# Loading scale, shift and the first product's weights interleaved by k-tile, with eight blocks of that product beside the load

## The chip, the cores and the metric

The kernel runs on one core of one Trainium2 chip. The metric is the device time of one execution in microseconds (us), the median of several runs. Differences of about 0.2% can be measured here.

## The reference

Two layers work on x (256 tokens, 2048 channels, float32), both conditioned on a vector c. From c come, for each layer, six vectors of 2048 (shift, scale and gate, twice):

```
mod = silu(c) @ w_ada[i] + b_ada[i]
sh1, sc1, gt1, sh2, sc2, gt2 = split(mod, 6)
h = rms_norm(x, pre_mix_g[i]) * (1.0 + sc1) + sh1
y = conformer_conv(h, ...)        # layer 0
...
x = x + gt1 * rms_norm(y, post_mix_g[i])
h = rms_norm(x, pre_ffn_g[i]) * (1.0 + sc2) + sh2
x = x + gt2 * rms_norm(swiglu_ffn(h, ...), post_ffn_g[i])
```

The convolution module of layer 0 is `u = h @ w_pw1 + b_pw1` (2048 to 4096), `a * sigmoid(g)` of its halves, a causal depthwise convolution with 31 taps over the tokens, layer norm, silu, and a second product `@ w_pw2`. Layer 1 has gated linear attention in its place. Both end in a SwiGLU network of width 5632.

## The kernel before, in words

**Layout.** Channels lie on the partitions, tokens along the free axis: x is 16 k-tiles of 128x256. Weights stream in tiles of 1 MB, each holding 16 blocks of 128x128 in the order in which they are multiplied (`ORDERS`). ScalarE rounds each half tile to `hi` (L282), and GpSimd or VectorE makes `lo = raw - hi` (L283; GpSimd for all of pw1, the first product). A block is multiplied as hi times the activation's high half, hi times its low half, and lo times the high half: L314, L315 and L320 for a block with a bank half of 256 columns. There are three buffers for `hi` and three for `lo` (half tiles), and six for `raw`.

**Modulation vectors.** For shift and scale of the first layer (`ada` tiles) VectorE multiplies a tile of w_ada by silu(c) and accumulates along its free axis (L261); one tile gives one column, 128 values of mod. A bias is added (L267), and for a scale `chunk_done` makes `(1 + scale) * gain` (L204). `modulate` then makes the k-tile of h: VectorE (L388, which reads the spread root of x from PSUM), ScalarE (L391, the high half), VectorE (L392, the low half). Three other vectors of layer 0 (`adap` tiles) are made on TensorE (L215).

**The order of the work.** `tile_order` writes out one list of all transfers, issued by SP in that order: the 16 scale tiles, with the parameters behind the second and x behind the third of them; then the 16 shift tiles, with the first four tiles of pw1 among them; then the other 28 tiles of pw1 with 26 `adap` tiles spread between them, 10 more `adap` tiles, and the rest. The bias of the scale and its product with the gain come once, over 16 columns, when all 16 scale tiles are there; the shift is finished column by column. Within an engine, instructions are ordered ahead of time by the compiler's own schedule.

**The first product.** `block_order` puts the first `PW1_GROUP` = 4 of the 32 output blocks together: for each k, all four, so that they advance as h becomes ready. The other 28 blocks follow one by one, each over all 16 k. Output blocks come as pairs, 0 and 16, 1 and 17 and so on (value and gate of one channel tile). Each block has its own bank of PSUM out of four (`mm`). `conv_done` reads a finished block on ScalarE (L549 for the value, L554 for the gate's sigmoid; two buffers each), multiplies them into `up` (L556; on VectorE for the first two channel tiles, else on GpSimd; four buffers), and VectorE runs the taps one after the other in PSUM (L597, two buffers; for the last two tiles L578 with part of the taps on TensorE, L565). Behind the last tile stand the layer norm's statistics, its root on GpSimd (L354), and the second product.

Of the kernel before, what the change touches and what calls it, by code (L numbers as in the profile page):

```python
# [14 lines left out]
P = 128  # L15
# [12 lines left out]
EPS = 1e-6  # L28
GROUP = 4
# [11 lines left out]
PW1_GROUP = 4  # L41
# [11 lines left out]
def ffn_in_obs(half):  # L53
# [4 lines left out]
    "pw1": block_order(PW1_OBS, KD, PW1_GROUP),  # L58
# [24 lines left out]
def tile_order():  # L83
# [11 lines left out]
    order = ada(0, SC1)  # L95
    order[2:2] = [("par", 0, 0)]
    order[4:4] = [("x", 0, 0)]
    shift = ada(0, SH1)
    order += shift[:4] + pw1[:1] + shift[4:7] + pw1[1:2] + shift[7:10] + pw1[2:3] + shift[10:13] + pw1[3:4] + shift[13:]
    order += spread(pw1[PW1_GROUP:], late[:26]) + late[26:36]  # L100
# [23 lines left out]
def trunk(ctx: ExitStack, tc: tile.TileContext, a: dict, out: bass.AP):  # L124
# [74 lines left out]
    def chunk_done(layer, chunk):  # L199
        m = modcol(layer, chunk * KD, KD)  # L200
        kinds = {SC1: (0, "pre_mix_g"), GT1: (1, "post_mix_g"), SC2: (2, "pre_ffn_g"), GT2: (3, "post_ffn_g")}
        if chunk in kinds:
            kind, g = kinds[chunk]
            nc.vector.scalar_tensor_tensor(  # L204
                out=der[:, layer * 4 + kind, :], in0=m, scalar=1.0 if kind in (0, 2) else 0.0,
                in1=cols(g, layer * KD, KD), op0=ALU.add, op1=ALU.mult,
            )
# [30 lines left out]
    def pump_one():  # L238
# [19 lines left out]
        if kind == "ada":  # L258
# [5 lines left out]
            if i % KD == KD - 1 or (name, i // KD) == (0, SH1):  # L264
                first = i if i // KD == SH1 and name == 0 else i - KD + 1
                m = modcol(name, first, i + 1 - first)
                nc.vector.tensor_tensor(  # L267
                    out=m, in0=m, in1=cols("b_ada", name * 6 * KD + first, i + 1 - first), op=ALU.add
                )
                if i % KD == KD - 1:  # L270
                    chunk_done(name, i // KD)
            if (name, i // KD) == (0, SH1):
                modulate(i % KD, rbx, 0, 0, SH1)
# [27 lines left out]
    def product(name, kts, act, on_done, step=None, narrow=(), join=True):  # L301
        live = {}
        for idx, (ob, k) in enumerate(ORDERS[name]):
            if idx % HALF == 0:
                w_hi, w_lo = next_half()
            if ob not in live:
                live[ob] = [ps.tile([P, 512], F32, tag="mm", name=f"{name}_{ob}"), 0]
            acc, n = live[ob]
            s = slice((idx % HALF) * P, (idx % HALF + 1) * P)
            pair = act(k)  # L310
            x_hi, x_lo = pair[:, 0, :], pair[:, 1, :]
# [12 lines left out]
            if end:  # L324
                live.pop(ob)
                on_done(ob, acc[:, :T] if ob in narrow else joined(ob, acc) if join else acc)
                if step is not None:
                    step()
# [600 lines left out]
```

## Time and profile before

| What | Value |
|---|---|
| Median of 3 runs | 2474.18 us (2470.78 to 2474.72) |
| Span of the profiled execution | 2464.2 us |
| Own time of the profiled execution | not given beside the span; the median is 9.98 us above the span |
| Mean granted TensorE clock | 0.983 |
| TensorE / VectorE / ScalarE / GpSimd busy | 95% / 75% / 45% / 11% of the span |
| DMA | 604.32 MB, mean 245 GB/s |

Times in the profile are microseconds from the span's start. "Busy" of TensorE counts matmuls that overlap, so one of 0.28 us may follow another after 0.12. A row of the timeline is: start, duration, engine, line, operation, what it writes and reads, how many are merged, and in brackets how long the engine had been idle and what released it. A row of a group is: count, then total busy time and mean nanoseconds of one, then idle time ahead of them and who ended it. A row of a stretch gives its bounds, its length, then busy time of TensorE, its weight loads, VectorE, ScalarE and GpSimd, the granted clock, the share of the DMA engines and GB/s. A row of the waits gives who waited for whom, total, times and the longest. A row of one line's durations gives minimum, median and maximum in nanoseconds.

### The profile page before, as it was taken

To read this page: it belongs to the slowest core of one execution; us is meant where nothing else is said; L and a number is where in the kernel's file an instruction comes from. 1 tells how busy PE (TensorE), PEld (TensorE's weight loads), DVE (VectorE), ACT (ScalarE), POOL (GpSimd) and SP (SyncE) were. 2 spreads that over 40 slices of the span, in tenths; PEclk is the share of its full clock that TensorE was granted. 3 is DMA by queue.
4 is the path that set the end of the run, shared out by engine and by line. 5 is a ranking of instruction groups with operands and counts; after the bars stand their busy time and mean duration, and the time that the engine had idled before them with its cause. 6 is when DMAs were issued, how large, how long until landed. Compare 5 with 4: busy or idle time off the path is not lost.

```text
span 2464.2 us, 35791 instructions
## 1 busy us (share of the span) xinstructions
PE 2341.2 (95%) x14170; PEld 2025.0 (82%) x14170; DVE 1854.2 (75%) x2778; ACT 1120.2 (45%) x1703; POOL 275.6 (11%) x148
## 2 busy tenths in 40 slices
PE   3699999999999999999989999997999999999997
PEld 2588756778888888888879989986888888888886
DVE  7988878787787677778977888799666655665665
ACT  2243426554444444444445445454544444444442
POOL 0377731120000000000030000003000000000001
PEclk9899999999999999999989999998999999999998
DMA  9877786547777777877733666773566656665651
GB/s 398 337 269 270 263 350 250 211 165 297 292 292 292 287 292 294 312 294 289 296 110 138 221 256 238 283 290 115 187 224 226 224 203 222 218 221 203 222 188 69
DMA packets 84155, 604.32 MB, mean 245 GB/s; under 512 B 9473, under 2 KB 9857, under 8 KB 11025
## 3 DMA queue, kind: packets, MB, share of 16 engines
q1 hardware_dynamic: 83986, 602.02, 65.7%
q8 instruction: 111, 1.82, 0.3%
q14 instruction: 58, 0.48, 0.1%
HBM read 599.89 MB, written 2.10 MB: 244 GB/s over the span
## 4 chain that ended last, share of the span: by engine, by line
PE 88%; DVE 9%; DMA 1%; issue 1%; POOL 1%; ACT 1%; SPq 0%; POOLq 0%; ACTq 0%; DVEq 0%
PE in L317 26%; PE in L320 13%; PE out L317 13%; PE out L320 7%; PE pw L320 3%; PE pw L314 3%; PE pw L315 2%; PE wo L317 2%; DVE h L392 2%; PE pw L317 2%; PE ada L215 2%; DVE raw L261 2%; PE r L315 1%; PE r L314 1%; PE r L320 1%; PE v L796 1%
## 5 line engine op out<-in xcount | busy, mean ns | idle before, releaser
L282 ACT CAST hi<-raw 128x1024 fp32r<-128x1024 f32 x754 | 790.6, 1049 | 1050.7 <-issue 299.9
L283 DVE TENSOR_TENSOR lo<-raw,hi 128x1024 fp32r<-128x1024 f32 x660 | 807.2, 1224 | 480.3 <-ACT hi L282 478.5
L317 PE MATMUL in<-h,hi 128*128 128x512 f32 x2816 | 987.3, 397 | 16.2 <-DVE h L392 15.8
L320 PE MATMUL in<-h,lo 128*128 128x256 f32 x2816 | 784.4, 279 | 0.0
L317 PEld LDWEIGHTS in<-h,hi 128*128 128x128 f32 x2816 | 529.7, 188 | 147.8 <-DVE h L392 16.4
L320 PEld LDWEIGHTS in<-h,lo 128*128 128x128 f32 x2816 | 531.1, 189 | 0.0
L317 PE MATMUL out<-m,hi 128*128 128x512 f32 x1364 | 477.2, 394 | 0.0
L320 PE MATMUL out<-m,lo 128*128 128x256 f32 x1408 | 391.9, 281 | 0.0
L283 POOL TENSOR_TENSOR lo<-raw,hi 128x1024 fp32r<-128x1024 f32 x94 | 232.7, 2480 | 1099.1 <-ACT hi L282 1079.7
L261 DVE SCALAR_TENSOR_TENSOR raw<-raw,cb 128x2048 f32<-128x2048 f32 x144 | 328.8, 2286 | 12.7 <-ACT cb L153 8.1
L317 PEld LDWEIGHTS out<-m,hi 128*128 128x128 f32 x1364 | 254.9, 188 | 58.5
L320 PEld LDWEIGHTS out<-m,lo 128*128 128x128 f32 x1408 | 264.1, 188 | 2.0
L320 PE MATMUL pw<-h,lo 128*128 128x256 f32 x768 | 218.0, 291 | 2.9 <-POOL lo L283 2.9
L597 DVE SCALAR_TENSOR_TENSOR ca<-up,dw,ca 128x256 f32<-128x256 f32 x420 | 170.9, 484 | 24.4 <-ACT ca L595 23.0
L314 PE MATMUL pw<-h,hi 128*128 128x256 f32 x528 | 155.7, 303 | 32.6 <-ACT hi L282 28.2
L315 PE MATMUL pw<-h,hi 128*128 128x256 f32 x528 | 154.4, 295 | 11.4 <-DVE h L392 11.4
L320 PEld LDWEIGHTS pw<-h,lo 128*128 128x128 f32 x768 | 148.8, 197 | 13.2 <-issue 6.2
L314 PEld LDWEIGHTS pw<-h,hi 128*128 128x128 f32 x528 | 103.9, 201 | 60.5 <-ACT hi L282 29.3
L315 PEld LDWEIGHTS pw<-h,hi 128*128 128x128 f32 x528 | 105.6, 201 | 14.2 <-DVE h L392 13.3
L317 PE MATMUL pw<-h,hi 128*128 128x512 f32 x240 | 85.7, 403 | 1.7 <-DVE h L383 1.7
L391 ACT ACTIVATE h<-mt,mod 128x256 fp32r<-128x256 f32 x64 | 31.7, 507 | 120.7 <-DVE mod L267 74.0
L317 PE MATMUL wo<-oo,hi 128*128 128x512 f32 x240 | 83.7, 394 | 0.0
(302 smaller groups left out, 2642.3 us busy)
## 6 DMA issues: line engine op xcount, KB each, us to landing
raw<-in_in_dram SPq DMA_DIRECT2D x176, 1024.0 KB, 4.9
raw<-in_w_ada_dram SPq DMA_DIRECT2D x144, 1024.0 KB, 5.3
raw<-in_out_dram SPq DMA_DIRECT2D x88, 1024.0 KB, 4.9
raw<-in_pw_dram SPq DMA_DIRECT2D x48, 1024.0 KB, 6.9
raw<-in_w_ada_d_dram SPq DMA_DIRECT2D x48, 1024.0 KB, 6.2
raw<-in_aqk_dram SPq DMA_DIRECT2D x17, 1024.0 KB, 4.8
raw<-in_v_dram SPq DMA_DIRECT2D x16, 1024.0 KB, 5.1
raw<-in_r_dram SPq DMA_DIRECT2D x16, 1024.0 KB, 5.5
```

What stands on the lines that cost most here:

```text
L215: nc.tensor.matmul(rows[n][32 * j : 32 * j + 32, :], cc[:, k, :], raw[:, j * 512 : (j + 1) * 512], start=k == 0, stop=k == KD - 1,)
L261: nc.vector.scalar_tensor_tensor(out=raw, in0=raw, scalar=1.0, in1=cb, op0=ALU.mult, op1=ALU.mult, accum_out=modcol(name, i))
L282: nc.scalar.copy(hi, part)
L283: done = eng.tensor_tensor(out=lo, in0=part, in1=hi.bitcast(F32), op=ALU.subtract)
L314: nc.tensor.matmul(acc[:, :T], w_hi[:, s], x_hi, start=n == 0, stop=False)
L315: nc.tensor.matmul(acc[:, :T], w_hi[:, s], x_lo, start=False, stop=False)
L317: nc.tensor.matmul(acc, w_hi[:, s], pair.rearrange("p a b -> p (a b)"), start=n == 0, stop=end, skip_group_check=True)
L320: nc.tensor.matmul(acc[:, :T], w_lo[:, s], x_hi, start=False, stop=end, skip_group_check=ob not in narrow)
L391: nc.scalar.activation(out=h_hi[:, k, :], in_=t, func=AF.Identity, bias=sh)
L392: return nc.vector.scalar_tensor_tensor(out=h_lo[:, k, :], in0=t, scalar=sh, in1=h_hi[:, k, :].bitcast(F32), op0=ALU.add, op1=ALU.subtract)
L597: nc.vector.scalar_tensor_tensor(out=ca, in0=u[:, w : w + T], scalar=cw, in1=ca, op0=ALU.mult, op1=ALU.add)
L796: nc.tensor.matmul(accs[t], h_hi[:, k, c], w_hi[:, s], start=k == 0, stop=False)
```

## The change

Four things change, all ahead of the second product.

1. The list of transfers begins with the parameters, the first scale tile, x and the first shift tile. Then scale and shift tiles alternate by k, and after each two k comes one tile of pw1: eight of them in all.
2. The scale is finished like the shift, column by column: bias, product with the gain, and modulation for each k.
3. The first eight output blocks of pw1 (four pairs) advance together by k, in place of four.
4. These eight are packed two to a bank, so that they need the same four banks; a pair is handed on when both of its blocks are finished.

```
-PW1_GROUP = 4
+HEAD = 8
...
-    "pw1": block_order(PW1_OBS, KD, PW1_GROUP),
+    "pw1": block_order(PW1_OBS, KD, HEAD),
...
+    scale, shift = ada(0, SC1), ada(0, SH1)
+    order = [("par", 0, 0), scale[0], ("x", 0, 0), shift[0]]
+    for i in range(HEAD):
+        order += [scale[2 * i + 1], shift[2 * i + 1]]
+        order += [scale[2 * i + 2], shift[2 * i + 2]] if 2 * i + 2 < KD else []
+        order += [pw1[i]]
+    order += spread(pw1[HEAD:], late[:26]) + late[26:36]
...
-    def chunk_done(layer, chunk):
-        m = modcol(layer, chunk * KD, KD)
+    def chunk_done(layer, chunk, first=0, n=KD):
+        m = modcol(layer, chunk * KD + first, n)
...
+            chunk, k = divmod(i, KD)
+            single = name == 0 and chunk in (SC1, SH1)
+            if single or k == KD - 1:
+                first = k if single else 0
+                m = modcol(name, chunk * KD + first, k + 1 - first)
...
+                chunk_done(name, chunk, first, k + 1 - first)
+            if name == 0 and chunk == SH1:
+                modulate(k, rbx, 0, 0, SH1)
...
+        def packed_block(ob, k, w_hi, w_lo, x_hi, x_lo):
+            bank, half = seats[ob]
+            if bank not in banks:
+                banks[bank] = ps.tile([P, 512], F32, tag="mm", name=f"{name}_pair{bank}")
+            acc = banks[bank][:, half * T : (half + 1) * T]
+            opens, closes = k == 0 and half == 0, k == kts - 1
+            nc.tensor.matmul(acc, w_hi, x_hi, start=opens, stop=False, skip_group_check=True)
+            nc.tensor.matmul(acc, w_hi, x_lo, start=False, stop=False, skip_group_check=True)
+            nc.tensor.matmul(acc, w_lo, x_hi, start=False, stop=closes, skip_group_check=True)
+            if closes:
+                finished.setdefault(bank, []).append((ob, acc))
+                if half:
+                    banks.pop(bank)
+                    for pair in finished.pop(bank):
+                        done(*pair)
...
-        product("pw1", KD, h_act, conv_done, narrow=range(2 * KD))
+        product("pw1", KD, h_act, conv_done, narrow=range(2 * KD), packed=HEAD * KD)
```

More of the change, by code (lines that the diff above doesn't have):

```diff
@@ L94, in tile_order @@
     late = adap(*PE_CHUNKS)
[L95 to L100, printed above, removed]
+    scale, shift = ada(0, SC1), ada(0, SH1)
[5 more added lines that the diff above has]
+    order += spread(pw1[HEAD:], late[:26]) + late[26:36]
     order += spread(pw2[:10], late[36:]) + pw2[10:]
@@ L204, in chunk_done @@
             nc.vector.scalar_tensor_tensor(
-                out=der[:, layer * 4 + kind, :], in0=m, scalar=1.0 if kind in (0, 2) else 0.0,
-                in1=cols(g, layer * KD, KD), op0=ALU.add, op1=ALU.mult,
+                out=der[:, layer * 4 + kind, first : first + n], in0=m, scalar=1.0 if kind in (0, 2) else 0.0,
+                in1=cols(g, layer * KD + first, n), op0=ALU.add, op1=ALU.mult,
             )
@@ L299, in next_half, with product, done @@
         return halves.pop(i)
-    def product(name, kts, act, on_done, step=None, narrow=(), join=True):
+    def product(name, kts, act, on_done, step=None, narrow=(), join=True, packed=0):
         live = {}
+        seats = {}
+        for ob, _ in ORDERS[name][:packed]:
+            seats.setdefault(ob, divmod(len(seats), 2))
+        banks, finished = {}, {}
+        def done(ob, acc):
+            on_done(ob, acc)
+            if step is not None:
+                step()
+        def packed_block(ob, k, w_hi, w_lo, x_hi, x_lo):
[13 more added lines that the diff above has]
+                        done(*pair)
         for idx, (ob, k) in enumerate(ORDERS[name]):
@@ L305, in product @@
                 w_hi, w_lo = next_half()
+            s = slice((idx % HALF) * P, (idx % HALF + 1) * P)
+            pair = act(k)
+            x_hi, x_lo = pair[:, 0, :], pair[:, 1, :]
+            if ob in seats:
+                packed_block(ob, k, w_hi[:, s], w_lo[:, s], x_hi, x_lo)
+                continue
             if ob not in live:
@@ L308, in product @@
             acc, n = live[ob]
-            s = slice((idx % HALF) * P, (idx % HALF + 1) * P)
-            pair = act(k)
-            x_hi, x_lo = pair[:, 0, :], pair[:, 1, :]
             end = n == kts - 1
@@ L325, in product @@
                 live.pop(ob)
-                on_done(ob, acc[:, :T] if ob in narrow else joined(ob, acc) if join else acc)
-                if step is not None:
-                    step()
+                done(ob, acc[:, :T] if ob in narrow else joined(ob, acc) if join else acc)
     def h_act(k):
@@ L490, in trunk @@
     ssx = None
-    pump(-1)
-    while order[state["next"]][0] != "w" and order[state["next"]] != ("ada", 0, SH1 * KD):
+    while order[state["next"]] != ("ada", 0, SH1 * KD):
         pump_one()
@@ L780, in step @@
                             diagonal(h)
-            product("aqk", KD, h_act, aqk_done, step, narrow=range(2*KK+1))
+            product("aqk", KD, h_act, aqk_done, step, narrow=range(2 * KK + 1))
             accs = {}
```

9 lines of the change are left out of this document (1 added, 8 removed).

## Prediction

> **What bounds the kernel now.** I read the page first, then the windows around the edited part, then engine by engine what ends each wait there.
>
> ```profile
> span 2464.2 us, 35791 instructions
> ```
> ```profile
> core 0: us, PE busy (x) PEld busy (x) DVE busy (x) ACT busy (x) POOL busy (x), PEclk, DMA share, GB/s
> 10.00:54.00 44.00, 15.23 (x66) 14.34 (x66) 37.42 (x37) 11.30 (x34) 2.70 (x1) 1.00 1.01 421
> 54.00:122.00 68.00, 36.83 (x178) 32.42 (x179) 66.22 (x80) 16.52 (x25) 22.42 (x8) 0.84 0.86 344
> 122.00:347.00 225.00, 224.37 (x1693) 179.44 (x1692) 186.42 (x452) 87.94 (x133) 153.12 (x83) 1.00 0.75 283
> ```
>
> The sum is made against the profiled span, 2464.2 us. The median of the runs is 2474.18, so 10.0 us lie around the span; I carry them over unchanged. About 5 us, 0.2%, is what a measurement of this kernel can tell from no change.
>
> The table shows two stages. Up to 122 us VectorE is the limit: 37.4 of 44 us while the DMA runs at 421 GB/s, then 66.2 of 68 us while the DMA has slack (0.86). From 122 to 347 us TensorE is busy for 224.4 of 225 us and VectorE only for 186.4. The border is the last modulation (the low half of h, k = 15); the far end is the last sigmoid of the first product and the tail behind it:
>
> ```profile
> 121.29 0.48 DVE L392 SCALAR_TENSOR_TENSOR h<-mt,mod,h 128x256 fp32r<-128x256 f32 x1 [0.58 <-ACT h L391]
> ```
> ```profile
> 346.99 0.48 ACT sg L554
> ```
> ```profile
> 362.33 0.70 POOL nl_r L354
> ```
>
> So the first stage ends at 121.8, the product at 347.0, and the layer norm's root starts at 362.3. That TensorE really sets the pace of the second stage, and isn't merely shown busy, follows from what it feeds on: the rounding copies on ScalarE wait for TensorE to give buffers back, not the other way round, and matmuls follow each other at 0.12 us.
>
> ```profile
> ACT hi L282 <- PE pw L315: 106.1, 46, 5.2
> ```
> ```profile
> 319.15 0.12 PE pw L320
> 319.27 0.12 PE pw L314
> ```
>
> **The product: what leaves the second stage.** One weight tile holds 16 blocks of 128x128, each used by three matmuls, so it costs 16 x 3 x 0.12 = 5.8 us of TensorE. Before, 4 of the 32 tiles are multiplied before the border; after, 8. Four tiles leave the bound stage: 4 x 5.8 = 23.0 us. The 26 ada tiles spread through it and the 10 behind them are the same number of matmuls as before and stay. The extra four tiles fit below VectorE's cover in the first stage: TensorE is busy 36.8 of 68 us there, and 23 us more at the fast pace (up to 40 at the slower granted clock of 0.84 and below) still leaves it below VectorE. If that cover were gone, part of the 23 us would only be moved. Packing two blocks into one bank changes no matmul; a bank is now free only after a pair's two readings on ScalarE, at most 1 us more once, at the border. So the second stage is 22 to 23 us shorter, provided VectorE can follow:
>
> ```profile
> L597 DVE SCALAR_TENSOR_TENSOR ca<-up,dw,ca 128x256 f32<-128x256 f32 x420 | 170.9, 484 | 24.4 <-ACT ca L595 23.0
> ```
> ```profile
> L556 DVE TENSOR_TENSOR up<-xa,sg 128x256 f32<-128x256 f32 x2 | 3.0, 1504 | 4.6 <-ACT sg L554 4.6
> ```
> ```profile
> 131.15 25.04 DVE L597 SCALAR_TENSOR_TENSOR ca<-up,dw,ca 128x256 f32<-128x256 f32 x62
> ```
>
> Taps follow at 25.04/62 = 0.40 us. All 420 of L597, and 26 of L578 for the last block but one (31 without 4 on TensorE and one on ScalarE), are 446 x 0.40 = 178 us; with 4.6 us until the first can start and 3.0 us of products u (L556), VectorE is done 186 us behind the border. TensorE hands over the last pair 225 - 23 = 202 us behind it. VectorE's margin is 16 us: it isn't the bound, but nearly.
>
> **The load: what the first stage gains in work.** Four more weight tiles mean eight more subtractions on GpSimd (L283) inside the time in which VectorE is the limit. These are the dearest part of the change, and the reason is in these rows:
>
> ```profile
> 91.12 2.28 DVE L261 SCALAR_TENSOR_TENSOR raw<-raw,cb 128x2048 f32<-128x2048 f32 x1
> 93.33 0.08 DVE L261 DVE_READ_ACCUMULATOR raw<-raw,cb 128x1 f32 x1
> 93.33 2.55 DVE L392 SCALAR_TENSOR_TENSOR h<-mt,mod,h 128x256 fp32r<-128x256 f32 x1
> 95.80 2.32 DVE L267 TENSOR_TENSOR mod<-mod,par 128x1 f32<-128x1 f32 x1
> ```
> ```profile
> 92.31 5.79 POOL L283 TENSOR_TENSOR lo<-raw,hi 128x1024 fp32r<-128x1024 f32 x2 [8.00 <-ACT hi L282]
> ```
> ```profile
> 122.27 4.75 POOL L283 TENSOR_TENSOR lo<-raw,hi 128x1024 fp32r<-128x1024 f32 x2 [10.39 <-ACT hi L282]
> ```
> ```profile
> 62.77 0.16 DVE L267 TENSOR_TENSOR mod<-mod,par 128x1 f32<-128x1 f32 x1
> 62.84 0.48 DVE L388 SCALAR_TENSOR_TENSOR mt<-x,der,nx_rb 128x256 f32<-128x256 f32 x1
> ```
> ```profile
> 79.50 0.48 DVE L388 SCALAR_TENSOR_TENSOR mt<-x,der,nx_rb 128x256 f32<-128x256 f32 x1
> ```
>
> An addition of one column takes 0.16 us at 62.77 and 2.32 at 95.80, where GpSimd subtracts; L392 takes 2.55 there against 0.48 at the border. L388, one of whose inputs lies in PSUM, keeps its 0.48 while GpSimd runs (at 79.50). And it goes both ways: the GpSimd pair at 92.31 took 5.79, 1.04 more than the undisturbed 4.75, which is the time until the running L261 ended (92.31 to 93.33). So the two engines exclude each other, one whole instruction at a time, where VectorE reads two tiles from SBUF. The sum of what that costs is in the groups of the stretch 53.2 to 118, which holds all eight subtractions:
>
> ```profile
> L283 POOL TENSOR_TENSOR lo<-raw,hi 128x1024 fp32r<-128x1024 f32 x8 | 22.4, 2822 | 52.9 <-ACT hi L282 52.9
> ```
> ```profile
> L392 DVE SCALAR_TENSOR_TENSOR h<-mt,mod,h 128x256 fp32r<-128x256 f32 x14 | 14.7, 1055 | 0.9 <-ACT h L391 0.9
> ```
> ```profile
> L267 DVE TENSOR_TENSOR mod<-mod,par 128x1 f32<-128x1 f32 x15 | 11.0, 732 | 0.0
> ```
>
> Undisturbed, L392 would have taken 14 x 0.48 = 6.7 and L267 15 x 0.16 = 2.4. The excess is 8.0 + 8.6 = 16.6 us, 2.1 us for each subtraction. Eight more cost 16.6 us. Lower bound: if all 16 L388, the only longer work that runs beside GpSimd, at 0.40 each, fell into such stretches, 6.4 us less, 10.2. Upper bound: 8 x 2.4 (half of 4.75), 19.
>
> The scale is now finished per k-tile: 16 additions (L267) and 16 products (L204) of one column, for one of each over 16 columns. VectorE's cost for such steps:
>
> ```profile
> 53.20 0.17 DVE L267 TENSOR_TENSOR mod<-mod,par 128x16 f32<-128x16 f32 x1
> 53.41 0.17 DVE L204 SCALAR_TENSOR_TENSOR der<-mod,par 128x16 f32<-128x16 f32 x1
> 53.70 0.48 DVE L388 SCALAR_TENSOR_TENSOR mt<-x,der,nx_rb 128x256 f32<-128x256 f32 x1
> ```
>
> Not waiting for each other they start 0.07 apart (62.77 to 62.84); each waiting for the one ahead, 0.21 and 0.29. So 32 x 0.07 = 2.2 at least and 16 x 0.50 = 8 at most; I take 5, between them, since other ready work will stand between some of them. No further wait is added by this: behind the small step on VectorE stands only the next L261, whose tile is already there.
>
> x moves from the fourth large transfer to the second, past two scale tiles on SP's queue, so the root of x is spread over the partitions earlier than its present 38 us:
>
> ```profile
> 4.08 13.14 DMA x<-in_x_dram
> ```
> ```profile
> 37.06 1.22 PE L370 MATMUL nx_rb<-nx_dg,ones 128*128 128x256 f32 x2 [3.49 <-DVE nx_dg L359]
> ```
> ```profile
> raw<-in_pw_dram SPq DMA_DIRECT2D x48, 1024.0 KB, 6.9
> ```
>
> x now lands at 17.2. With two tiles of 1024 KB (1.05 MB) less ahead of it, at 421 GB/s, that is 5 us earlier. This moves modulations forward, but removes no VectorE work; its idle time before 54 us is 44 - 37.4 = 6.6 us, set by tiles of 1.05 MB that arrive every 2.5 us against 2.29 us of work. What it can give: part of the small steps and the first two subtractions now fall into this idle time. I take 2 us off, bounds 0 and 6. The DMA doesn't become the limit: 40 tiles x 2.5 us and x are 105 us, all under VectorE's time.
>
> Sum for the border: 16.6 + 5 - 2 = 19.6 later, say 19 (it is 10.2 + 2.2 - 6 = 6 at least, 19 + 8 = 27 at most): 121.8 becomes 141. The product's end: 347 - 23 + 19 = 343. The tail behind it (15.3 us of taps, last block) is unchanged, and so is everything later. **Net: 4 us less**, 2470. The gain of TensorE is nearly all given back on VectorE. By the bounds the net lies between -17 and +5.
>
> One row speaks for a cheaper load:
>
> ```profile
> L261 DVE SCALAR_TENSOR_TENSOR raw<-raw,cb x144: 2283/2286/2293, 10.4 to 2318.0; 128x2048 f32<-128x2048 f32 x144
> ```
>
> L261 is never stretched in 144 times. In the rows it always came first, so they don't show whether it can start beside a running subtraction; if it can, the 16.6 us mostly fall away (rival A).
>
> The Trainium skill, SBUF — State Buffer, Who interferes with whom, says that a VectorE instruction with two SBUF inputs and a GpSimd instruction that reads SBUF block each other fully, whichever starts second, for the other's whole length. By that rule L261 has to wait too when it comes second, no order of VectorE's queue escapes, and the border comes 19 us later, not 3; the 2.55 us of L392 and the 1.04 us that GpSimd waited for L261 agree with it.
>
> **The rivals.**
> A, the subtractions hide. If L261 can start beside a running subtraction (it was never seen stretched), or if VectorE waits for tiles when GpSimd runs, the eight more cost nothing: the border moves by 5 - 2 = 3, and the net is -23 + 3 = -20: 2454. For it: the row above. Against it: GpSimd did wait for L261 at 92.31, and VectorE has only 6.6 us to wait in. Chance 0.15.
>
> B, slower: GpSimd's queue stops at the fifth pair. Four pairs now come to the convolution at once. The product u of pair 4 writes the buffer whose first user is pair 0, and the taps of pairs 0 and 1 run interleaved:
>
> ```profile
> 138.46 0.47 ACT L554 ACTIVATE sg<-pw,par 128x256 f32<-128x256 f32 x1
> ```
> ```profile
> 152.82 0.38 ACT L600 COPY uc<-ca 128x256 f32<-128x256 f32 x1
> ```
>
> The first sigmoid of a pair not held over the border comes 16.7 us behind it; the first taps are done 31 us behind it. So u of pair 4 waits 14 us, and if it stands in GpSimd's queue ahead of the next subtractions, TensorE runs out of low halves: three buffers of 24 matmuls, 2.9 us each, cover 3 to 6 of the 14. A price of 8 to 11 us; net +7: 2481. It decides from 9 us on. Against it: subtractions have nothing to wait for, and can be queued ahead of u. Chance 0.2.
>
> C, VectorE becomes the bound of the convolution: if its 24.4 us of waits for the first tap on ScalarE (row of L597) stay, its 186 us become 210, 8 behind TensorE's 202. Net +4: 2478. Against it: these waits come from pairs not yet being there, and four are in stock now. Chance 0.1.
>
> D, the change does less than it says: TensorE multiplies the extra four blocks only after the border. Then 23 us are not gained while the load is 19 longer: 2493. Against it: TensorE has 31 us free there, and for each k it needs 24 matmuls, 2.9 us, while VectorE has two L261 of 2.3, L388, L392 and a stall of 2.1, together over 7. Chance 0.03.
>
> **How the numbers follow.** The forecast, with the remaining chance 0.52, is 2470, its own range 2458 to 2479; inside it I give 0.42 to faster by over 0.2% (the stalls or the small steps cost 1 us less than taken and the gain passes 5), 0.52 to within 0.2%, 0.06 to slower. Faster: 0.52 x 0.42 + 0.15 = 0.37. Slower: 0.03 from the forecast, 0.17 from B, 0.03 from C, 0.03 from D: 0.26. Within: the rest, 0.37. The range goes from 2455, which leaves out half of A, to 2483, which leaves out the dear end of B, and D.
>
> **What would show it.** Right: the last L392 of the first layer between 134 and 147 us; sixteen subtractions ahead of it and L392, L267, L204 or L261 stretched to over 2 us some fourteen times; the last sigmoid of the product 199 to 204 us behind the border; VectorE without waits for ScalarE's first taps until late. Wrong: a border before 128 (A); TensorE idle with GpSimd as releaser 17 to 31 us behind the border (B); the last sigmoid more than 208 us behind it (B, C, D). A change of more than 5 us behind 400 us would be outside my reasons.

## The result, and the profile after

The kernel after takes 2485.58 us (median of 4 runs, 2480.2 to 2487.28), the kernel before 2472.48 (4 runs, 2466.72 to 2474.72). The ratio is 1.0051, 95% interval 1.0037 to 1.0065: slower by half a per cent, where 4 us less was forecast. The profiled execution of after has a span of 2478.3 us, that of before 2464.2: 14.1 us to explain.

First the border, which is the end of the load: the last modulation in VectorE's timeline, and the next thing that VectorE does (start, duration, line, and in brackets the idle time ahead with what ended it).

```profile
140.64 0.48 DVE L421 SCALAR_TENSOR_TENSOR h<-mt,mod,h 128x256 fp32r<-128x256 f32 x1 [0.58 <-ACT h L420]
151.18 0.43 DVE L584 TENSOR_TENSOR up<-xa,sg 128x256 f32<-128x256 f32 x1 [10.06 <-ACT sg L582]
```

The load ends at 141.1 us, 19.3 later than before, where 19 was forecast. Then ScalarE's timeline, the first result of the first product and the sigmoid of its last one, and GpSimd's, the root of the layer norm behind it; the third fence is the first result of before:

```profile
148.90 0.47 ACT L577 ACTIVATE xa<-pw_pair,par 128x256 f32<-128x256 f32 x1 [1.63 <-PE pw_pair L323]
...
347.19 0.47 ACT L582 ACTIVATE sg<-pw,par 128x256 f32<-128x256 f32 x1 [1.09 <-PE pw L351]
```
```profile
380.66 0.70 POOL L383 TENSOR_TENSOR nl_r<-l_v,mhalf 128x2 f32<-128x2 f32 x1 [16.36 <-DVE l_v L656]
```
```profile
124.06 0.47 ACT L549 ACTIVATE xa<-pw,par 128x256 f32<-128x256 f32 x1 [0.92 <-PE pw L320]
```

From the first result to the last sigmoid it is 198.3 us; before it was 222.9 (124.06 to 346.99). The product is 24.6 us shorter, near the 23 of the forecast. But the last sigmoid comes no earlier, and the root, 15.3 us behind it before, now comes 33.5 us behind it. So the loss is 18.3 us at the root. Behind it 5.0 us are won back up to the next norm (380.7 to 495.2 us, before 362.3 to 481.9), and from there all marks are 13 to 14 us later.

Where the 18 us of the tail sit is read from the busy times of three stretches: load, product, tail. First after, then before:

```profile
core 0: us, PE busy (x) PEld busy (x) DVE busy (x) ACT busy (x) POOL busy (x), PEclk, DMA share, GB/s
54.00:141.20 87.20, 45.17 (x243) 42.69 (x242) 82.66 (x99) 15.61 (x22) 31.16 (x10) 0.69 0.86 325
141.20:347.20 206.00, 202.81 (x1532) 159.59 (x1530) 164.54 (x410) 80.08 (x122) 136.96 (x75) 0.99 0.76 286
347.20:380.70 33.50, 21.14 (x123) 9.15 (x122) 29.74 (x74) 9.01 (x15) 4.79 (x5) 0.71 0.87 345
```
```profile
121.30:347.00 225.70, 225.07 (x1696) 180.13 (x1695) 186.90 (x453) 88.64 (x133) 153.12 (x83) 0.99 0.75 283
347.00:362.30 15.30, 13.51 (x83) 7.18 (x82) 12.65 (x32) 6.71 (x10) 0.73 (x1) 1.00 0.83 316
```

VectorE's work behind the border is nearly the same: 164.5 + 29.7 = 194.3 us, before 186.9 + 12.7 = 199.6. What has not become less is its idle time during the product: 206.0 - 164.5 = 41.5 us, before 38.8. By these rows the stretch from the border to the last sigmoid became 19.7 us shorter, VectorE stood idle as long as before in it, so 17.1 us more of its work lies behind the last sigmoid (29.7 instead of 12.7). From the border to the root it takes 240 us, as before (241). VectorE's waits in that stretch, after and then before (total, times, longest):

```profile
DVE ca L625 <- ACT ca L623: 21.8, 7, 6.1
DVE up L584 <- ACT sg L582: 10.1, 1, 10.1
DVE uc L610 <- PE pt L593: 5.2, 1, 5.2
DVE mod L229 <- PE adac L227: 4.5, 2, 3.3
```
```profile
DVE ca L597 <- ACT ca L595: 23.0, 9, 4.3
DVE mod L228 <- PE adac L226: 8.2, 2, 4.7
DVE up L556 <- ACT sg L554: 4.6, 1, 4.6
```

The waits for the first tap on ScalarE (L623) are as long as before, although four pairs are in stock at the border. The start costs 5.5 us more (10.1 instead of 4.6), and one reason is that the product starts again late: the low half of the last weight tile is made behind the border. GpSimd's timeline, all subtractions from the first one on, and TensorE's:

```profile
30.93 4.83 POOL L285 TENSOR_TENSOR lo<-raw,hi 128x1024 fp32r<-128x1024 f32 x2
46.12 5.28 POOL L285 TENSOR_TENSOR lo<-raw,hi 128x1024 fp32r<-128x1024 f32 x2 [10.37 <-ACT hi L284]
65.82 6.23 POOL L285 TENSOR_TENSOR lo<-raw,hi 128x1024 fp32r<-128x1024 f32 x2 [14.42 <-ACT hi L284]
82.09 6.23 POOL L285 TENSOR_TENSOR lo<-raw,hi 128x1024 fp32r<-128x1024 f32 x2 [10.04 <-ACT hi L284]
98.36 6.24 POOL L285 TENSOR_TENSOR lo<-raw,hi 128x1024 fp32r<-128x1024 f32 x2 [10.04 <-ACT hi L284]
114.62 6.23 POOL L285 TENSOR_TENSOR lo<-raw,hi 128x1024 fp32r<-128x1024 f32 x2 [10.03 <-ACT hi L284]
130.89 6.23 POOL L285 TENSOR_TENSOR lo<-raw,hi 128x1024 fp32r<-128x1024 f32 x2 [10.04 <-ACT hi L284]
141.62 9.43 POOL L285 TENSOR_TENSOR lo<-raw,hi 128x1024 fp32r<-128x1024 f32 x4 [4.50 <-ACT hi L284]
```
```profile
144.06 0.39 PE L323 MATMUL pw_pair<-h,lo 128*128 128x256 f32 x1 [1.16 <-POOL lo L285]
```

So fourteen subtractions lie ahead of the border, and not the sixteen of eight tiles; before it was eight.

The load as a whole lost what the prediction said it would, but not all of it as forecast. VectorE's work in the load (after, then before) grew by 15.2 us and its idle time by 4.2 (131.1 - 118.8 = 12.3, before 8.2):

```profile
10.00:141.10 131.10, 74.85 (x397) 70.77 (x398) 118.79 (x146) 33.14 (x65) 41.94 (x15) 0.79 0.90 354
```
```profile
10.00:121.80 111.80, 51.86 (x243) 46.56 (x244) 103.64 (x116) 27.62 (x59) 25.12 (x9) 0.90 0.92 374
```

While GpSimd's pair at 82.09 runs, VectorE's steps of one column take the length of a subtraction; in the groups of the whole load these small steps cost 959 and 471 ns on the mean instead of some 160. With one L421 and one `nx_dg` of 2.6 to 2.7 us, thirteen instructions are stretched there, by 27.2 us in all; before it was eight, by 16.6:

```profile
83.84 2.17 DVE L270 TENSOR_TENSOR mod<-mod,par 128x1 f32<-128x1 f32 x1
86.05 2.29 DVE L205 SCALAR_TENSOR_TENSOR der<-mod,par 128x1 f32<-128x1 f32 x1
```
```profile
L205 DVE SCALAR_TENSOR_TENSOR der<-mod,par 128x1 f32<-128x1 f32 x16 | 15.3, 959 | 0.5
L270 DVE TENSOR_TENSOR mod<-mod,par 128x1 f32<-128x1 f32 x32 | 15.1, 471 | 0.6
```

### The profile page after: what moved, and what is told of

It is laid out like the page before. It is cut to its first block, busy times and chain, and to the rows that moved or that the text cites. A ratio compares the mean times of both kernels' runs of the same rounds, so it can differ in the third digit from the quotient of the medians.

```text
span 2478.3 us, 35802 instructions
## 1 busy us (share of the span) xinstructions
PE 2348.5 (95%) x14170; PEld 2034.6 (82%) x14170; DVE 1862.2 (75%) x2808; ACT 1119.9 (45%) x1703; POOL 277.2 (11%) x148
## 4 chain that ended last, share of the span: by engine, by line
PE 87%; DVE 7%; issue 3%; POOL 2%; DMA 1%; ACT 1%; SPq 0%; POOLq 0%; ACTq 0%
PE in L348 26%; PE in L351 13%; PE out L348 13%; PE out L351 7%; PE pw L351 3%; PE wo L348 2%; PE pw L345 2%; PE pw L348 2%; PE pw L346 2%; PE ada L216 2%; DVE h L421 1%; PE r L346 1%; PE r L345 1%; PE r L351 1%; PE v L826 1%
## 5 line engine op out<-in xcount | busy, mean ns | idle before, releaser
L348 PEld LDWEIGHTS in<-h,hi 128*128 128x128 f32 x2816 | 530.4, 188 | 145.0 <-DVE h L421 14.5
L262 DVE SCALAR_TENSOR_TENSOR raw<-raw,cb 128x2048 f32<-128x2048 f32 x144 | 329.0, 2285 | 11.4 <-ACT cb L154 8.2
L625 DVE SCALAR_TENSOR_TENSOR ca<-up,dw,ca 128x256 f32<-128x256 f32 x420 | 168.9, 482 | 22.6 <-ACT ca L623 21.8
L351 PE MATMUL pw<-h,lo 128*128 128x256 f32 x640 | 179.9, 283 | 0.0
L351 PEld LDWEIGHTS pw<-h,lo 128*128 128x128 f32 x640 | 121.3, 190 | 6.9 <-issue 3.3
L345 PE MATMUL pw<-h,hi 128*128 128x256 f32 x400 | 116.9, 292 | 0.0
L346 PE MATMUL pw<-h,hi 128*128 128x256 f32 x400 | 113.7, 284 | 0.0
L345 PEld LDWEIGHTS pw<-h,hi 128*128 128x128 f32 x400 | 76.3, 191 | 23.5 <-issue 21.3
L346 PE MATMUL aqk<-h,hi 128*128 128x256 f32 x272 | 77.9, 293 | 4.9 <-DVE h L421 4.8
```

Of the source, the lines that this page charges most:

```text
L262: nc.vector.scalar_tensor_tensor(out=raw, in0=raw, scalar=1.0, in1=cb, op0=ALU.mult, op1=ALU.mult, accum_out=modcol(name, i))
L345: nc.tensor.matmul(acc[:, :T], w_hi[:, s], x_hi, start=n == 0, stop=False)
L346: nc.tensor.matmul(acc[:, :T], w_hi[:, s], x_lo, start=False, stop=False)
L348: nc.tensor.matmul(acc, w_hi[:, s], pair.rearrange("p a b -> p (a b)"), start=n == 0, stop=end, skip_group_check=True)
L351: nc.tensor.matmul(acc[:, :T], w_lo[:, s], x_hi, start=False, stop=end, skip_group_check=ob not in narrow)
L625: nc.vector.scalar_tensor_tensor(out=ca, in0=u[:, w : w + T], scalar=cw, in1=ca, op0=ALU.mult, op1=ALU.add)
```

## The experiments

Two things had to be told apart. For the load: whether the 19 us come from the two engines shutting each other out, or from the new small steps, or from the order of the transfers. For the tail: theory A', that VectorE has the time for its taps but its queue, worked off in a fixed order, holds at its head an instruction that needs TensorE while ready taps stand behind it; or theory B, that there is too much work behind the border in whatever order; the first experiment asks for a third cause, too few accumulators. Each expectation says what the theories that it names hold. "Border" is the end of the last modulation, "tail" the time from the last sigmoid to the root.

| kernel | median us | ratio to before, 95% | border | last sigmoid | root |
|---|---|---|---|---|---|
| before | 2472.5 | 1 | 121.8 | 347.0 | 362.3 |
| after | 2485.6 | 1.0037 to 1.0065 | 141.1 | 347.2 | 380.7 |
| e1 four accumulators | 2485.6 | 1.0039 to 1.0070 | 141.5 | 341.0 | 379.6 |
| e2 low halves on VectorE | 2459.2 | 0.9936 to 0.9969 | 126.7 | 323.1 | 355.9 |
| e3 four blocks | 2479.1 | 1.0015 to 1.0035 | 122.6 | 353.5 | 368.8 |
| e4 old order | 2478.3 | 1.0014 to 1.0033 | 135.9 | 341.2 | 372.1 |
| e5 taps without ScalarE | 2482.2 | 1.0022 to 1.0052 | 141.9 | 345.5 | 377.9 |
| e6 small steps on ScalarE | 2475.2 | 1.0008 to 1.0026 | 133.3 | 337.4 | 370.9 |
| e7 weight tile earlier | 2484.7 | 1.0041 to 1.0071 | 148.0 | 346.4 | 379.7 |
| e8 before, as e5 | 2471.4 | 0.9988 to 1.0007 | 121.9 | 345.2 | 360.6 |
| e9 e5, columns elsewhere | 2482.6 | 1.0029 to 1.0063 | 142.2 | 345.9 | 377.9 |
| e10 e9 and e2 | 2461.2 | 0.9940 to 0.9970 | 126.2 | 323.4 | 358.3 |
| e11 before, as e2 | 2467.3 | 0.9973 to 0.9997 | 115.5 | 344.3 | 359.6 |
| e12 e10 and e6 | 2462.3 | 0.9948 to 0.9974 | 125.9 | 329.7 | 364.8 |
| e13 e9, PSUM sum last | 2482.2 | 1.0027 to 1.0061 | 140.9 | 344.6 | 377.0 |
| e14 e13 and e2 | 2461.6 | 0.9944 to 0.9973 | 126.5 | 323.8 | 359.3 |
| e15 before, as e14 | 2468.1 | 0.9970 to 0.9989 | 115.8 | 343.7 | 359.0 |
| e16 e13, tile 15 last | 2484.3 | 1.0034 to 1.0058 | 142.3 | 347.7 | 382.1 |
| e17 e16 and e2 | 2458.0 | 0.9929 to 0.9957 | 126.2 | 323.6 | 356.3 |
| e18 e17, no first taps on ScalarE | 2457.7 | 0.9937 to 0.9964 | 127.1 | 324.3 | 352.9 |

### The load

**e2, the subtractions ahead of the border on VectorE.**

```
-        on_pool = name == "pw1" or (name == "pw2" and ...
+        on_pool = (name == "pw1" and i >= HEAD) or (name == "pw2" and ...
...
-            last_lo[:] = [] if on_pool else [done.ins]
+            last_lo[:] = [] if on_pool or name == "pw1" else [done.ins]
```

> The changed kernel with the sixteen subtractions of the first eight weight tiles on VectorE instead of GpSimd. If the two engines exclude each other, sixteen stalls of 2.1 us (34 us) give way to sixteen subtractions of 1.22 us (20 us): the last modulation comes 14 us earlier, near 127 us, and with an unchanged tail the time falls by 12-16 us, to about 2471. If the small steps were stretched for another reason, VectorE has 20 us more to do and the border moves to 160.

The border comes 14.5 us earlier than in after, though VectorE now does sixteen subtractions more. Its groups in the load:

```profile
L285 DVE TENSOR_TENSOR lo<-raw,hi 128x1024 fp32r<-128x1024 f32 x16 | 18.9, 1218 | 0.0
...
L270 DVE TENSOR_TENSOR mod<-mod,par 128x1 f32<-128x1 f32 x32 | 4.8, 156 | 0.2
...
L205 DVE SCALAR_TENSOR_TENSOR der<-mod,par 128x1 f32<-128x1 f32 x16 | 2.5, 155 | 0.1
```

18.9 us of work replace 18.9 + 14.5 = 33.4 us of loss. Over the fourteen subtractions that stood in after's load this is 2.4 us each, near the 2.1 that the prediction read from before; it holds idle time of VectorE too (12.3 us in after's load, 6.9 here). The small steps are back at 0.16 us. This kernel, with two lines changed, beats both: 0.5% under before, 1.1% under after. The time fell by 26.4 us, not by the 12 to 16 expected: besides the border, the first sigmoid now comes 2.7 us behind it instead of 9.6, since the last tile's low half is made ahead of it. **e11** makes the same edit in before (eight subtractions).

> Control: the kernel before the change with the eight subtractions of its first four weight tiles on VectorE. Eight stalls of 2.1 us (17 us) for eight subtractions of 1.22 us (10 us): the border 7 us earlier, and the whole kernel 5-8 us faster, since TensorE sets the pace behind it: about 2466. If the exclusion costs less than measured, no change.

The border came 6.3 us earlier, near the 7 expected, and the time is 5 us lower by the medians (1 to 7 by the interval). So once the low halves are made on VectorE, the change itself is worth 8 us (2459.2 against 2467.3).

**e6, the 48 small steps on ScalarE.**

```
-                nc.vector.tensor_tensor(out=m, in0=m, in1=cols("b_ada", ...), op=ALU.add)
-                chunk_done(name, chunk, first, k + 1 - first)
+                nc.scalar.activation(out=m, in_=m, func=AF.Identity, bias=col("b_ada", ...))
+                if chunk == SC1:
+                    g = col("pre_mix_g", first)
+                    nc.scalar.activation(out=der[:, 0, first : first + 1], in_=m, func=AF.Identity, scale=g, bias=g)
```

> The changed kernel with the 48 one-column steps of the load (32 bias additions, 16 products with the gain) on ScalarE. If my term for them, 5 us and 1.6 us of before, was about right, the border comes 5-8 us earlier, at 134, and the time falls by as much. It also changes what VectorE starts beside a running subtraction: if the long L261 starts second there, it is stretched to over 4 us where the exclusion holds for it too, and stays at 2.29 us if it doesn't; in the latter case the border comes another 15 us or more earlier, before 122.

The border came 7.8 us earlier, and the time fell by 10.4. What the prediction could not see in before is now in the trace. L262, stretched in none of 144 cases before, with its shortest, median and longest duration in ns:

```profile
L262 DVE SCALAR_TENSOR_TENSOR raw<-raw,cb x144: 2275/2284/4426, 10.4 to 2325.3; 128x2048 f32<-128x2048 f32 x144
```

With the small steps out of the way the long instruction comes second, and waits 2.14 us as they did. So it isn't immune, and rival A falls; that it was never stretched before fits its always having come first. The Trainium skill, SBUF — State Buffer, Who interferes with whom, says that whichever of the two instructions starts second waits for the whole of the other; the 4.43 us agree with it.

**e4, eight blocks with the transfers in the old order** and the scale finished together.

```
+    order = scale[:2] + [("par", 0, 0)] + scale[2:3] + [("x", 0, 0)] + scale[3:] + shift[:1]
     for i in range(HEAD):
+        order += shift[2 * i + 1 : 2 * i + 3] + [pw1[i]]
```

> Eight blocks beside the load, but the transfers in the old order: all scale tiles, finished together, then the shift tiles with one weight tile after each two. This is the eight blocks alone. If the loss comes from the eight blocks (stalls in the load, a longer tail), the border comes at 121.8 + 16.6 = 138 us, the tail is over 28 us and the time is within 4 us of the changed kernel. If it came from the interleaving, the time is near that of the kernel before.

The border is 5.2 us better than after and the tail is still 30.8 us. The time was expected within 4 us of after; it is 7.3 us lower, and so nearer to before (5.9 us over it). GpSimd's timeline shows its pairs even longer than in after, each of the two subtractions waiting for VectorE in turn:

```profile
97.55 8.86 POOL L283 TENSOR_TENSOR lo<-raw,hi 128x1024 fp32r<-128x1024 f32 x2 [1.91 <-ACT hi L282]
```

**e3, the interleaved order with four blocks as before.**

```
-HEAD = 8
+HEAD = 4
-    for i in range(HEAD):
+    for i in range(KD // 2):
-        order += [pw1[i]]
+        order += [pw1[i // 2]] if i % 2 else []
```

> The changed kernel with four blocks (two pairs) beside the load: scale and shift still alternate and are finished by column, one weight tile after each four k. This is the interleaving alone. By the sum of the prediction the border comes at 121.8 + 5 - 2 = 125 us, the tail is 15 us as before the change, and the time is 2 to 4 us over the kernel before. If the interleaving itself is dear, the border is past 130 us; if the long tail has to do with the interleaving and not with the stock of pairs, it is over 25 us here too.

The border is 0.8 us later than before and the tail 15.3 us as before. So neither the late border nor the long tail comes from the interleaving and its small steps; eight blocks make both (e4). But in time the interleaving is not free: e3 alone costs 6 us over before, e4 alone 6 us, and after, with both, 13. The 6 us of e3 (2 to 4 were expected) come behind the border: its first sigmoid stands 12.3 us behind it (4.1 before), and ScalarE starts the last weight tile's rounding copies only at 121.95 us, behind its last modulation.

**e7, each weight tile ahead of its two k-tiles** (`order += [pw1[i]]` moved to the head of the loop), to take the late restart away.

> The changed kernel with each of the eight weight tiles two k earlier in the list of transfers, so that the last one isn't the last transfer of the load. If the 8 us between the last modulation and the product's first result (2.3 us before the change) come from the last tile being rounded and subtracted behind the last modulation, this gap falls to under 4 us and the last sigmoid comes 4-6 us earlier; the time falls by no more than 5 us, since VectorE's taps end the stage. If the gap has to do with the order on ScalarE's queue and not with the transfer, it stays at 8.

The first sigmoid comes 3.6 us behind the border instead of 9.6, but the border itself came 6.9 us later: the two subtractions shut VectorE out inside the load instead of standing behind it. The last sigmoid comes 0.8 us earlier, where 4 to 6 were expected, and nothing is won.

### The tail

**e1, four accumulators** for the taps instead of two, two to a PSUM bank.

```
-            ca = ps2.tile([P, 512], F32, tag="acc", name=f"ca{b}", bufs=2)[:, :T]
+            if b % 2 == 0:
+                duo[:] = [ps2.tile([P, 512], F32, tag="acc", name=f"ca{b}", bufs=2)]
+            ca = duo[0][:, (b % 2) * T : (b % 2 + 1) * T]
```

> The changed kernel with four tap accumulators in flight instead of two (two channel tiles share one bank). Theory 1: VectorE gets behind because only two accumulators exist and the first tap of the next ones stands behind a sigmoid on ScalarE, so that the stock of four pairs is not worked off while TensorE multiplies; then its waits for first taps fall from 21.8 us to under 8, the time from the last sigmoid to the layer norm's root falls from 33.5 to 15-20 us, and the time by about 15 us, to 2470. Theory 2: VectorE has simply too much work, or the order on its own queue holds it; then the accumulators change less than 4 us.

The waits for first taps went from 21.8 to 17.9 us, and the last sigmoid came 6.2 us earlier; but the root moved by only 1.1 us and the time not at all. Too few accumulators is not the cause.

**e5, ScalarE taken out of tiles 0 to 13**: first tap on VectorE, last tap written straight into uc.

```
-                if w == 0 and b < 2:
+                if w == 0:
...
-                elif w == 0:
-                    nc.scalar.activation(out=ca, in_=u[:, w : w + T], func=AF.Identity, scale=cw, bias=bias)
...
-                        out=ca, in0=u[:, w : w + T], scalar=cw, in1=ca, op0=ALU.mult, op1=ALU.add
+                        out=uc[:, b, :] if w == PAD else ca, in0=u[:, w : w + T], scalar=cw, in1=ca, op0=ALU.mult, op1=ALU.add
...
-            nc.scalar.copy(uc[:, b, :], ca)
```

> The changed kernel with VectorE's taps freed from ScalarE's queue: the first tap of every channel tile on VectorE, and the last tap of tiles 0 to 13 writes its sum straight to SBUF, in place of a copy on ScalarE. Four accumulators alone changed nothing, so the question is what holds VectorE back. Theory A, the queues: first taps and copies stand behind sigmoids on ScalarE; then the 21.8 us of waits for ScalarE fall below 6, the time from the last sigmoid to the layer norm's root falls from 33.5 to 16-22 us and the time by 10-15 us, to about 2473. Theory B, the work: VectorE has 193 us of work behind a start at 151 and can't end before; then the twelve first taps (0.45 us each) only add 5 us.

The 21.8 us of waits for ScalarE are gone, and this stands in their place among VectorE's waits:

```profile
DVE mod L229 <- PE adac L227: 20.1, 2, 17.3
```

L229 finishes a modulation that is needed much later; it needs TensorE, stands in VectorE's queue ahead of ready taps, and all of them wait 17.3 us with it. The tail is 32.4 us and the time 2482.2, so theory A of this run missed. **e8**, the same edit in before, changes nothing in the time.

> Control: the kernel before the change with the same edit to the taps as in the run of the changed kernel (first tap on VectorE, last tap straight to SBUF). Before the change VectorE waited 23.0 us for first taps too, but there because TensorE had not yet made the next pair: if so, nothing is gained, and the time is within 4 us of the kernel before. If ScalarE's queue cost time there as well, it is faster by more than 5 us.

There the waits only changed their name. They are now for `up`, made of the next pair right behind its sigmoid, which isn't there yet:

```profile
DVE ca L591 <- POOL up L556: 20.1, 4, 5.4
```

**e9** takes L229 off VectorE as well (a copy on ScalarE, additions and products on GpSimd), and **e13** besides adds TensorE's part of tile 14 last instead of first:

```
-                    nc.vector.tensor_tensor(out=uc[:, b, :], in0=pt, in1=base, op=ALU.subtract)
-                    for o in parts:
+                    head, rest = (pt, parts) if last else (ca, [pt])
+                    nc.vector.tensor_tensor(out=uc[:, b, :], in0=head, in1=base, op=ALU.subtract)
+                    for o in rest:
```

> The changed kernel with the taps freed from ScalarE's queue as before, and in addition the finishing of TensorE's modulation columns (a sum and a product over 16 columns, which wait for TensorE in the middle of the taps) on ScalarE and GpSimd. In the run without ScalarE in the taps, VectorE got ahead and then stood 17.3 us at such a sum, with taps ready behind it. Theory A', VectorE's own in-order queue: with these out of it VectorE isn't held, its idle time between the border and the layer norm falls below 18 us (10 at the start, 5 at the first TensorE taps), the time from last sigmoid to root falls from 33 to 15-20 us, and the time to about 2470. Theory B, the work: the root comes within 4 us of the run before it.

> As the run with the queue freed (changed kernel, taps without ScalarE, modulation columns off VectorE), and tile 14's sum reads TensorE's taps last instead of first, so that no instruction that waits for TensorE stands ahead of ready taps. Theory A', the order of VectorE's queue: the 18.8 us of waiting at that reading go; VectorE reaches the last sigmoid with only the taps of tiles 14 and 15 left; the stretch to the root falls from 32 to 18-24 us and the time by 8-14 us, to about 2471. Theory B, the work: the stretch stays over 29 us.

Both missed. VectorE's waits, the longest of e9 and of e13:

```profile
DVE uc L615 <- PE pt L598: 18.8, 1, 18.8
```
```profile
DVE cb L611 <- ACT cb L606: 22.2, 1, 22.2
```

Each time nearly all of the idle time is back (39 to 41 us from border to root in e5, e9 and e13; 45 in after), half of it at the next instruction of the queue that needs TensorE: first the sum of TensorE's taps, then tile 15's second accumulator, with taps of tiles 12 to 14 behind it. **e16** puts all of tile 15 behind tile 14 by giving it tile 14's accumulator:

```
+            ca = first.get("ca")
+            if ca is None:
+                ca = ps2.tile([P, 512], F32, tag="acc", name=f"ca{b}", bufs=2)[:, :T]
+            if b == KD - 2:
+                first["ca"] = ca
...
-                    if last:
-                        parts.append(ps.tile([P, 512], F32, tag="mm", name=f"cb{b}")[:, :T])
...
-                    head, rest = (pt, parts) if last else (ca, [pt])
+                    head, rest = ca, [pt]
```

> The kernel after with the edits of the run in which no instruction in VectorE's queue waits for TensorE ahead of ready taps of tiles 0 to 13, and with one more: tile 15 uses tile 14's accumulator and has no second one, so that all its taps and its last additions stand in VectorE's queue behind those of tile 14 (18 taps of about 0.39 us stay behind the last sigmoid instead of 44). Theory A' (VectorE has the time for all taps of tiles 0 to 14 ahead of the last sigmoid, and only its fixed order keeps it from using it): the 22.2 us wait for tile 15's first tap shrinks to under 8 us, tiles 12 to 14 are done at about 342 us, the layer norm's root comes 11 to 15 us behind the last sigmoid instead of 32.4, at about 358 us instead of 377.0, and the time is 2463 to 2469 us (2482.2 without this edit; some 5 us of the gain may be lost in the next stage, as the kernel after won about as much back there). Theory B (VectorE has too much work behind the border, in whatever order): the root stays 28 to 35 us behind the last sigmoid and the time is 2479 to 2484 us.

Missed again: the root came at 382.1, not 358. VectorE's timeline, and ScalarE's ahead of the same moment:

```profile
329.18 0.48 DVE L631 SCALAR_TENSOR_TENSOR uc<-up,dw,ca 128x256 f32<-128x256 f32 x1
349.20 3.64 DVE L613 SCALAR_TENSOR_TENSOR ca<-up,dw,ca 128x256 f32<-128x256 f32 x7 [19.54 <-POOL mod L232]
```
```profile
347.67 0.47 ACT L587 ACTIVATE sg<-pw,par 128x256 f32<-128x256 f32 x1 [2.17 <-PE pw L356]
348.46 0.17 ACT L231 COPY mod<-adac 128x16 f32<-128x16 f32 x1 [0.31 <-PE adac L228]
348.53 0.58 ACT L608 ACTIVATE ca<-up,par,dw 128x256 f32<-128x256 f32 x1
```

The profile names GpSimd as what ended the wait, but what L613 continues is the first tap of tile 14, L608 on ScalarE; it stands there behind tile 15's sigmoid and starts at 348.53. The wait had moved into the queue of another engine.

**e10, e14, e15, e17**: e9, e13, e13 in before and e16, with e2's edit in each.

> The same with the sixteen subtractions of the first eight weight tiles on VectorE. If the two losses (34 us of exclusion for 20 us of work in the load; VectorE's queue behind it) are separate, their gains add: 14 us and the gain of the run before. From 2485: to 2455 or so. If VectorE's taps end the stage by their number, the 14 us earlier border still moves it whole.

> The same with the sixteen subtractions of the head on VectorE. Under A' both gains add: border near 126, root near 345, time about 2448, faster than every run so far. Under B it stays with the run that has the queue freed and the subtractions moved, 2461.

> Control: the kernel before the change with all these edits (its eight subtractions on VectorE, taps without ScalarE, modulation columns off VectorE, tile 14 reading last). It has no stock of pairs to work off, so only the subtractions should count: 2467, as with them alone. If the queue cost it time too, it is below 2462.

> The same edit on the kernel that also makes the sixteen subtractions ahead of the border on VectorE (2461.6 us without this edit, with a wait of 20.3 us at tile 15's second accumulator). Theory A': the wait goes, the root comes 11 to 15 us behind the last sigmoid instead of 35.5, at about 340 us instead of 359.3, and the time is 2443 to 2450 us. Theory B: 2459 to 2464 us.

The tails are 34.9, 35.5, 15.3 and 32.7 us, and e10, e14 and e17 can't be told from e2 (their intervals overlap). So the gain in the tail that e10 and A' in e14 and e17 asked for did not come; the control e15 came near its 2467. **e12**, with e6's edit on top of e10, adds nothing, where 4 to 7 us were expected; its border comes 0.3 us earlier:

> The changed kernel with all three edits: subtractions of the head on VectorE, taps and modulation columns out of the queues that held them, and the 48 one-column steps of the load on ScalarE. The last were worth 8 us of the border with the exclusion in place (10 us of the time); without it I expect 5-7 us of the border, so 4-7 us less than the run with two of the edits. If TensorE's or the DMA's pace is reached in the load (40 tiles of 2.5 us and x: not before 108 us), less.

**e18** takes the last two first taps off ScalarE, and moves two subtractions of the next product, which stood among tile 14's taps, to GpSimd:

```
-        on_pool = ... (name == "pw2" and 1 <= i < POOL_TILES) ...
+        on_pool = ... (name == "pw2" and i < POOL_TILES) ...
...
-                            nc.scalar.activation(
-                                out=o, in_=u[:, w : w + T], func=AF.Identity, scale=cw,
-                                bias=bias if w == pe_taps else 0.0,
+                            nc.vector.tensor_scalar(
+                                out=o, in0=u[:, w : w + T], scalar1=cw, scalar2=bias, op0=ALU.mult, op1=ALU.add
                             )
```

> The kernel of the run just before (2458.0 us; VectorE done with tiles 0 to 13 at 308.6 us, then 16.5 us without work, because tile 14's first tap stands in ScalarE's queue behind tile 15's sigmoid), with the first taps of tiles 14 and 15 on VectorE, and the two subtractions of the next product's first weight tile, which stood between tile 14's taps, on GpSimd. Nothing in VectorE's queue now needs TensorE ahead of tile 15. Theory A' (only the fixed order of the queues keeps VectorE from using its time): tile 14 is done at about 324 us (308.7 + 27 taps of 0.52 us + 0.8), tile 15 at about 336 us (324.9 + 19 of 0.52 + 0.9), the root at about 340 us instead of 356.3, and the time is 2442 to 2448 us. Theory B (too much work behind the border, in whatever order, or some wait not seen yet): the root stays at 352 us or later and the time is 2454 to 2460 us.

Half of it came as A' had it. VectorE's timeline:

```profile
323.96 0.42 DVE L619 TENSOR_TENSOR uc<-pt,uc 128x256 f32<-128x256 f32 x1
325.62 0.55 DVE L608 TENSOR_SCALAR ca<-up,dw,par 128x256 f32<-128x256 f32 x1 [1.24 <-POOL up L589]
...
336.18 0.42 DVE L619 TENSOR_TENSOR uc<-pt,uc 128x256 f32<-128x256 f32 x1
350.57 0.42 DVE L649 COPY l_flat<-lstat 128x256 f32<-128x256 f32 x1 [13.96 <-PE lstat L574]
```

Tile 14 is done at 324.4 (324 expected) and tile 15 at 336.6 (336): 12.3 us behind the last sigmoid. So VectorE does have the time: that there is too much work for it falls. By root and time B's side came all the same, through its second reading, a wait not seen yet: the root stays at 352.9, because the sums over the last tiles stand in TensorE's queue behind two groups that wait for transfers, at a time when the DMA engines are busy for 0.99 of it (last row: the DMA share and GB/s at its end):

```profile
342.72 1.94 PE L216 MATMUL ada<-raw,cc 128*32 128x512 f32 x8 [5.03 <-DMA raw<-in_w_ada_d_dram]
347.71 1.93 PE L216 MATMUL ada<-raw,cc 128*32 128x512 f32 x8 [3.06 <-DMA raw<-in_w_ada_d_dram]
349.43 0.63 PE L574 MATMUL lstat<-uc,mean_w 128*32 128x256 f32 x1
```
```profile
310.00:350.00 40.00, 31.24 (x224) 17.59 (x216) 23.51 (x49) 8.65 (x14) 12.19 (x10) 0.89 0.99 398
```

The time, 2457.7 us, can't be told from that of e17 and e2. What stays open is whether the last 14 us come back when these groups stand behind the sums: that was not tried, and with the DMA this busy the next product's weights may simply be late instead.

## Why the prediction was wrong

**The border: right in its number, in part by luck.** 141.1 us for 141. The mechanism holds: each stretched instruction costs 2.1 us (27.2 us for thirteen, read from before as 16.6 for eight), and e11 gains 6.3 us by eight subtractions that cost 1.22 us each instead, so 2.0 us each. But "eight more" was wrong: the last tile's two subtractions fall behind the border, so there are six more, and the term of 16.6 us came out as 10.6. The small steps cost about the 5 us taken (15.2 of added work less 10.6). VectorE's idle time, which was to give 2 us, grew by 4.2. Two terms missed, by 6 us each, in opposite directions. With all sixteen ahead of the border (e7) it came at 148.0.

**Product shorter by 23 us: right for TensorE's own work** (24.6 from first to last result), but the stretch from border to last sigmoid, for which it was forecast, shrank by only some 19: the last sigmoid came 206 us behind the border, not 202. The product starts again some 5 us later, with the last tile's low half made behind the border. The prediction allowed 1 us at the border, for the handing on of a pair.

**"VectorE's margin is 16 us: it isn't the bound, but nearly" and "The tail behind it (15.3 us of taps, last block) is unchanged": these are the steps that failed.** The 186 us were work plus the wait for the first pair; the other waits were left out, on the ground that pairs in stock would take them away. They stayed: 41.5 us idle in the product, 38.8 before. So nearly all of the 19.7 us by which the product became shorter was handed on to the tail, which grew from 15.3 to 33.5 us. From border to root it took 240 us (194.3 of work and 45 idle), as before (241: 199.6 and 41), and the root came at 380.7 instead of the 358 that the forecast amounts to (343 + 15.3). Rival C named this mechanism, but kept only the 24.4 us at the first tap and so got 8 us for what became 18, and had 0.1 of the chance.

Its reason against, "four are in stock now", missed what the rows of the experiments show: the stock lies in the queue behind an instruction that waits, for ScalarE's first tap, itself behind a sigmoid; with that gone (e5) behind L229; then (e9) behind TensorE's sum; then (e13) behind tile 15; then (e16) behind ScalarE again. In before the same time went by for pairs that were not made yet (e8). e18 shows that without these waits VectorE is done 12 us behind the last sigmoid, and shows TensorE's queue as the next in the way; that the order of the queues is all that costs the 18 us is not shown.

**The other rivals.** A fell with e6. B did not come: TensorE waits for GpSimd only 1.2 us in the whole product. D did not come: TensorE resumed with only the last tile's products left. Far behind the tail nothing new came, as the prediction said: from 495 us on all marks are 13 to 14 us later.

## What to carry to other kernels

Before an engine is called "not the bound" because its work is less than another's, ask of each of its waits what ends it and what stands behind it in the queue. A wait does not go because ready work is in stock, if that work stands behind the waiting instruction; in after, e5, e9, e13 and e16 the idle time from border to root was 39 to 45 us, before 41. When a wait at a queue's head is removed, read the queue on to the next instruction that needs the same partner, in all engines' queues, before counting the gain. And a subtraction moved off the limiting engine is no gain if the two engines shut each other out: here 1.2 us on VectorE replaced 2.0 (e11) to 2.4 us (e2) lost beside GpSimd.

## What the runs showed of the hardware

The mutual exclusion of VectorE and GpSimd can appear almost wholly on the short instructions: in after, eleven steps of 0.16 us took 2.2 to 2.3 us, and the instruction of 2.28 us was never stretched until the short ones had gone to another engine (e6, 4.43 us). The loss was 2.1 us for each stretched instruction in before and after; for each subtraction on GpSimd it was 1.9 to 2.4 us, by whether VectorE's idle time is counted. GpSimd paid as well: a pair of 4.75 us took 6.23 in after and 8.86 in e4, where VectorE's instructions came between its two halves.
